# Hybrid encoder block on one core: down projection with tokens as rows, and projections of the merge in the wide form

## The chip, the cores and the metric

The kernel runs on one core of a Trainium2 chip. The metric is the device time of a run in microseconds. The engines are TensorE (PE, matmuls; PEld its weight loads), VectorE (DVE), ScalarE (ACT), GpSimd (POOL) and SyncE (SP), whose queue issues nearly all DMAs. Each works through its own list of instructions in order and waits on semaphores for the others.

## The reference

One layer over 256 tokens of width 2048, all in float32 (the weights and norms are drawn wider than here, which changes no shape):

```python
h = rms_norm(x, norm1_g)
proj = h @ w_in                      # u_a, v_a, feat_b, gate_a, gate_b
y_a = sgu_mixer(u_a, v_a, ...)       # spatial gating, width 1024
y_b = rwkv_mixer(feat_b, ...)        # two RWKV-7 scans, width 1024
merged = sigmoid(gate_a) * (y_a @ w_proj_a) + sigmoid(gate_b) * (y_b @ w_proj_b)
x = x + merged @ w_out
h2 = rms_norm(x, norm2_g)
gt = dwconv3_centred(h2 @ ffn_w_gate, ffn_conv_w, ffn_conv_b)
x = x + (silu(gt) * (h2 @ ffn_w_up)) @ ffn_w_down      # 5632 -> 2048
return rms_norm(x, norm_f_g)
```

## The kernel before

Activations lie feature by feature: a tile holds 128 features on the partitions and the 256 tokens as columns (P = 128, T = 256, KT = 16 tiles of the width 2048, FT = 44 of the width 5632, NP = 8 of the width 1024). Every large product is a *job* (`push`, L185): one tile of 128 output features, summed over nk tiles of input features. Its weights come in *chunks* of four 128x128 blocks, 256 KB each, which SP loads into a tile raw (`load_to`, L209).

To keep float32 precision with the faster fp32r matmul, each operand is the sum of a high and a low part. For the weights `split_to` (L216) makes them: ACT casts raw into hl[:, 0] (L223), DVE writes the rest into hl[:, 1] (L224). Activations are split in the same way when they are made (`split`, L172, and `split_scaled`, L176). `advance` (L228) takes one chunk at a time: it splits HL_AHEAD = 3 chunks ahead and issues the matmuls of the chunk, with the weights as the stationary and the activations as the moving operand. Low times low is left out. There are two forms:

- wide: high weights times high and low activations side by side (512 columns, L242), then low weights times high activations (256 columns, L246); two weight loads for 768 columns. The two halves of the result are added afterwards by `evac_sum` (L255: ACT copy L258, DVE add L259).
- narrow: three matmuls of 256 columns into one half (L244 to L246); three weight loads, nothing to add afterwards.

PE's work is thus one long row of jobs, and the rest of the kernel runs beside it in callbacks (`done`), called when a job's last matmul is issued. The stages, in order: projections of w_in with the RWKV and SGU work interleaved (wide; the gates' results, and branch A's times its gate, go to DRAM as spill); then the *merge*: the branch-B projection w_pb (16 jobs of 8 units, narrow, `done_b` L953) makes mg, the output projection w_out (16 jobs of 16 units, narrow, `done_o` L1007) adds x and makes h2 and the sum of squares for its norm; gate and up projections (88 wide jobs, `done_g`, `done_u`) make act; the *down* projection w_d (16 jobs of 44 units, the last one narrow, `done_d` L1053) adds into x2, which stays feature by feature. A unit is one 128x128 block with its two or three matmuls.

The final norm needs the sum of squares over all features, that is over partitions and tiles: `sumsq_rstd` (L980) adds squares tile by tile and sums over the partitions by a matmul with ones (L989, L990); then come, for each half of the tokens, the reciprocal root (`rsqrt`, L162) as a tile of 128x128, three multiplies (L1066) and three output DMAs (L1068).

From the merge on, raw has 8 buffers (RAW2) and is loaded 6 chunks ahead. The tile framework orders the instructions of each engine by its own estimates, so where a callback's work stands among the casts and subtracts of hl is not what the source alone shows.

## Time and profile before

| | us |
|---|---|
| median of 3 runs | 1582.59 (1581.76 to 1582.97) |
| profiled execution, its own time | 1567.25 |
| its span, first to last instruction | 1565.5 |
| PE busy in it | 1531.2 (98%) |
| DVE, ACT, POOL busy | 1222.2, 922.6, 37.9 |
| mean granted clock of TensorE | 0.996 |

The profile is one execution under the hardware profiler. Its spans on PE are pipelined: a matmul's duration overlaps the next one's, so a rate is read from the distance between starts. "Idle before" names what released an engine that had waited. The stages after the RWKV work lie, in us from the start of the span, at about 676 to 725 (branch B), 725 to 815 (output projection), 815 to 1304 (gate and up), 1304 to 1549 (down), and 1549 to the end (norm and output).

### The profile page before, as it was taken

Reading aid. Unit: us, or ns where it says so; the run is one execution under the profiler, and the core shown is the slowest. Engines: PE = TensorE matmul, PEld = TensorE weight load, DVE = VectorE, ACT = ScalarE, POOL = GpSimd, SP = SyncE. Lnnn points to the kernel's source line nnn. Section 1 sums busy time; section 2 is a strip of 40 time slices with the busy share of each in tenths; the row PEclk is TensorE's granted clock in tenths of the full one; section 3 lists DMA queues with packets and bytes.
Section 4 is the critical chain, followed back from the end, with each engine's and each line's share of the span. In section 5 each row is a group of like instructions: output and inputs, shape, how many; then the busy total and the mean of one; then the engine's idle time right before and its main releaser. Section 6 shows DMA issues by size and latency. Waiting matters only on the chain.

```text
span 1565.5 us, 35582 instructions
## 1 busy us (share of the span) xinstructions
PE 1531.2 (98%) x13420; PEld 1333.2 (85%) x13420; DVE 1222.2 (78%) x2500; ACT 922.6 (59%) x1920; POOL 37.9 (2%) x65
## 2 busy tenths in 40 slices
PE   6999999999999999999999999999999999999996
PEld 5888888888888878899998888888888888888885
DVE  8879998889898897687678777777787776555554
ACT  5667765665666655555556666666666665545452
POOL 2000000000000000000000000000000000000000
PEclk9999999999999999999999999999999999999998
DMA  6555553443443433597555555555555556666663
GB/s 230 195 181 177 166 160 126 132 144 120 135 140 116 139 100 124 161 316 240 187 182 188 194 190 189 189 192 190 190 189 189 190 191 191 189 191 190 190 190 100
DMA packets 151500, 273.72 MB, mean 175 GB/s; under 512 B 16928, under 2 KB 23200, under 8 KB 151328
## 3 DMA queue, kind: packets, MB, share of 16 engines
q1 hardware_dynamic: 148624, 263.91, 53.2%
q0 software_dynamic: 2560, 7.34, 1.4%
q8 instruction: 105, 1.72, 0.4%
q14 instruction: 67, 0.55, 0.1%
q10 hardware_dynamic: 144, 0.19, 0.0%
HBM read 265.09 MB, written 6.29 MB: 173 GB/s over the span
## 4 chain that ended last, share of the span: by engine, by line
PE 84%; issue 9%; DVE 4%; DMA 1%; ACT 1%; POOL 0%; SPq 0%; DVEq 0%; ACTq 0%; POOLq 0%
PE mm L242 45%; PE mm L246 26%; PE mm L244 3%; PE mm L245 3%; PE gp L669 1%; PE tp L717 1%; PE ms L541 1%; DVE hl L224 1%; DVE FQ L695 1%; PE tp L707 1%; PE cc L800 0%; DMA xt<-in_xT_dram 0%; PE tp L728 0%; DMA spill<-ev 0%; POOL spill L877 0%
## 5 line engine op out<-in xcount | busy, mean ns | idle before, releaser
L242 PE MATMUL mm<-h,hl 128*128 128x512 f32 x2624 | 935.7, 399 | 8.3 <-DVE h L178 7.6
L224 DVE TENSOR_TENSOR hl<-raw,hl 128x512 fp32r<-128x512 f32 x960 | 655.9, 689 | 231.0 <-ACT hl L223 227.3
L223 ACT CAST hl<-raw 128x512 fp32r<-128x512 f32 x960 | 594.7, 621 | 398.5 <-PE mm L246 284.9
L246 PE MATMUL mm<-h,hl 128*128 128x256 f32 x2624 | 733.3, 279 | 4.8 <-DVE hl L224 4.8
L242 PEld LDWEIGHTS mm<-h,hl 128*128 128x128 f32 x2624 | 493.2, 188 | 122.4 <-ACT hl L223 8.1
L246 PEld LDWEIGHTS mm<-h,hl 128*128 128x128 f32 x2624 | 495.0, 189 | 7.9 <-DVE hl L224 7.1
L242 PE MATMUL mm<-act,hl 128*128 128x512 f32 x660 | 228.8, 394 | 0.0
L246 PE MATMUL mm<-act,hl 128*128 128x256 f32 x704 | 195.3, 277 | 0.0
L242 PEld LDWEIGHTS mm<-act,hl 128*128 128x128 f32 x660 | 123.8, 188 | 28.7
L258 ACT COPY ev<-mm 128x256 f32<-128x256 f32 x180 | 67.1, 373 | 119.0 <-PE mm L246 118.7
L246 PEld LDWEIGHTS mm<-act,hl 128*128 128x128 f32 x704 | 132.4, 188 | 0.0
L259 DVE TENSOR_TENSOR ev<-mm,ev 128x256 f32<-128x256 f32 x180 | 75.9, 422 | 45.5 <-ACT ev L258 44.7
L246 PE MATMUL mm<-mg,hl 128*128 128x256 f32 x256 | 71.9, 281 | 0.0
L244 PE MATMUL mm<-mg,hl 128*128 128x256 f32 x256 | 71.7, 280 | 0.0
L245 PE MATMUL mm<-mg,hl 128*128 128x256 f32 x256 | 71.2, 278 | 0.0
L242 PE MATMUL mm<-ya,hl 128*128 128x512 f32 x128 | 48.2, 409 | 0.0
L244 PEld LDWEIGHTS mm<-mg,hl 128*128 128x128 f32 x256 | 48.1, 188 | 0.0
L245 PEld LDWEIGHTS mm<-mg,hl 128*128 128x128 f32 x256 | 48.1, 188 | 0.0
L246 PEld LDWEIGHTS mm<-mg,hl 128*128 128x128 f32 x256 | 48.1, 188 | 0.0
L1035 ACT ACTIVATE gt<-cp,colt 128x256 f32<-128x256 f32 x44 | 26.5, 603 | 19.1 <-DVE cp L1033 19.1
L246 PE MATMUL mm<-ybs,hl 128*128 128x256 f32 x128 | 36.2, 283 | 0.0
L245 PE MATMUL mm<-ybs,hl 128*128 128x256 f32 x128 | 36.2, 283 | 0.0
(285 smaller groups left out, 1523.6 us busy)
## 6 DMA issues: line engine op xcount, KB each, us to landing
raw<-in_w_in_dram SPq DMA_DIRECT2D x304, 256.0 KB, 3.0
raw<-in_w_g_dram SPq DMA_DIRECT2D x176, 256.0 KB, 3.1
raw<-in_w_u_dram SPq DMA_DIRECT2D x176, 256.0 KB, 2.9
raw<-in_w_d_dram SPq DMA_DIRECT2D x176, 256.0 KB, 2.9
raw<-in_w_out_dram SPq DMA_DIRECT2D x64, 256.0 KB, 3.0
raw<-in_w_pa_dram SPq DMA_DIRECT2D x32, 256.0 KB, 2.9
raw<-in_w_pb_dram SPq DMA_DIRECT2D x32, 256.0 KB, 4.7
spill<-ev POOLq DMA_DIRECT2D x32, 128.0 KB, 3.2
```

Source lines behind the costliest of these rows:

```text
L223: A.copy(hl[:, 0, :m], raw[:, s0:s0 + m])
L224: V.tensor_tensor(out=hl[:, 1, :m], in0=raw[:, s0:s0 + m], in1=hl[:, 0, :m].bitcast(F32), op=ALU.subtract)
L242: PE.matmul(ps[:, 0:512], hl[:, 0, j], a.rearrange("p a t -> p (a t)"), start=(k == 0), stop=False)
L244: PE.matmul(ps[:, 0:256], hl[:, 0, j], a[:, 0], start=(k == 0), stop=False)
L245: PE.matmul(ps[:, 0:256], hl[:, 0, j], a[:, 1], start=False, stop=False)
L246: PE.matmul(ps[:, 0:256], hl[:, 1, j], a[:, 0], start=False, stop=(k == job["nk"] - 1))
L258: A.copy(t, ps[:, 256:512])
L259: V.tensor_tensor(out=t, in0=ps[:, 0:256], in1=t, op=ALU.add)
L541: PE.matmul(ps[:, 0:T], bones, b[:, o], start=(o == 0), stop=(o == 1))
L669: PE.matmul(gps[hh][:, c * P:(c + 1) * P], BK[rows, d, c, hh:hh + 2, :].rearrange("p a b -> p (a b)"), AR[rows, d, c].rearrange("p a b -> ...
L695: V.copy_predicated(out=FQ2[qs, d, :, 1, :], mask=m2[qs, None, :].to_broadcast([32, NC, 32]), data=Gs[d][qs, q // 2, :, 0, b0:b0 + 32])
L1035: A.activation(gt, b[:, 1:T + 1], AF.Identity, scale=col("cw1", f), bias=col("cb", f))
```

## The change

The narrow form is given up in the merge: the jobs of w_pb and w_out are wide now, and `done_b` adds the halves with `evac_sum`.

The down projection turns its operands round. The activations act, a tile of 128 tokens at a time, become the stationary operand, and the split weights hl the moving one, 512 output features wide (WN): `push_tok` and `tok_mm`. A column group n of four takes 44 chunks, one per k; for each chunk there are three matmuls for token tile 0 and three for token tile 1, into two PSUM tiles pd0 and pd1. In the last group, token tile 1 runs up to LAG = 8 chunks behind token tile 0. The weights are laid out for this on the host, still 2 KB per partition and load.

The residual for the last addition must then have tokens as rows. x2 is no longer one tile for all features but six rotating ones, and `turn` transposes each of them on PE into x2t (two 128x128 transposes and one ACT copy per output job). `done_d` adds a result of 128x512 into x2t, squares it on ACT with a sum along the row, and lets GpSimd multiply by the norm's weights gf, which are loaded as one broadcast over the partitions. With the last group's result, the reciprocal root of a token tile is nine operations on one column (`rstd_of`); then ACT scales 768 columns and DVE 512 and 768, and two DMAs store the token tile.

RAW2 falls from 8 to 6, so 4 chunks are loaded ahead. The tiles h of the first projection are freed before the merge, and its small pools lie there. From the down projection on, hl has 4 + 9 buffers.

```diff
-RAW2 = 8
+RAW2 = 6
+
+WN = 512
+LAG = 8
+HL2 = 9
...
+    def push_tok(wd, nk, act, done, lag):
+
+
+        job = dict(wd=wd, nk=nk, act=act, done=done, ps=None, last=0, tok=True, lag=lag, at=0)
+        for k in range(nk):
+            raws.append([job, k, HK, None])
+            chunks.append([job, len(raws) - 1, 0, HK, None])
+        job["last"] = len(chunks)
+        jobs.append(job)
+        return job
+
+    def tok_mm(job, i):
+
+        if job["ps"] is None:
+            job["ps"] = [ps_d.tile([P, WN], F32, name=f"pd{t}", tag=f"pd{t}") for t in range(2)]
+        nk = job["nk"]
+        first = job["last"] - nk
+
+        def mm(t, k):
+            w = chunks[first + k][4].rearrange("p a b c -> p a (b c)")
+            a, ps, ts = job["act"](k), job["ps"][t], slice(t * P, t * P + P)
+            PE.matmul(ps, a[:, 0, ts], w[:, 0], start=(k == 0), stop=False)
+            PE.matmul(ps, a[:, 0, ts], w[:, 1], start=False, stop=False)
+            PE.matmul(ps, a[:, 1, ts], w[:, 0], start=False, stop=(k == nk - 1))
+            if k == nk - 1:
+                job["done"](t, ps)
+
+        k = i - first
+        mm(0, k)
+        upto = nk if k == nk - 1 else k + 1 - min(job["lag"], (k + 3) // 4)
+        while job["at"] < upto:
+            mm(1, job["at"])
+            job["at"] += 1
...
+            if r[0]["tok"]:
+                nc.sync.dma_start(r[3].rearrange("p a b -> p (a b)"), r[0]["wd"][:, r[1]])
+            else:
+                nc.sync.dma_start(r[3][:, :r[2]], r[0]["wd"][:, r[1]:r[1] + r[2]])
...
-            hl = hl_p.tile([P, 2, HK, P], F32R, name="hl", tag="hl")
+            hl = pools["hl"](ptr["hl"]).tile([P, 2, HK, P], F32R, name="hl", tag="hl")
...
+            if job["tok"]:
+                ptr["mm"] += 1
+                tok_mm(job, i)
+                continue
...
+    es_h.close()
...
-    x2 = xp_.tile([P, KT, T], F32, name="x2")
+
+    x2t = xp_.tile([P, 2, D], F32, name="x2t")
+    gf = xp_.tile([P, D], F32, name="gf")
+    ss = xp_.tile([P, 2, 8], F32, name="ss")
+    ps_d = ctx.enter_context(tc.tile_pool(name="ps_d", bufs=2, space=PSUM))
+    h2p = es_h2.enter_context(tc.tile_pool(name="h2p", bufs=1, reuse_waits="tile", side="right"))
+    h2 = [h2p.tile([P, 2, T], F32R, name=f"h2{m}") for m in range(KT)]
...
+            x2[m] = mgr.tile([P, T], F32, name="x2", tag="x2", bufs=X_AHEAD + 3)
+            nc.sync.dma_start(x2[m], xT[:, m])
...
-        V.scalar_tensor_tensor(out=sb, in0=sb, scalar=1.0, in1=ps, op0=ALU.add, op1=ALU.mult)
+        V.scalar_tensor_tensor(out=sb, in0=sb, scalar=1.0, in1=evac_sum(ev, ps), op0=ALU.add, op1=ALU.mult)
...
-        last_b = push(w_pb[m], NP, lambda k: ybs[k], lambda ps, m=m: done_b(m, ps), False)
+        last_b = push(w_pb[m], NP, lambda k: ybs[k], lambda ps, m=m: done_b(m, ps))
...
-        last_o = push(w_out[m], KT, lambda k: mg[k], lambda ps, m=m: lt["o"](m, ps), False)
+        last_o = push(w_out[m], KT, lambda k: mg[k], lambda ps, m=m: lt["o"](m, ps))
...
-    for m in range(KT):
-        last_d = push(w_d[m], FT, lambda k: lt["act"][k], lambda ps, m=m: lt["d"](m, ps), m < KT - 1)
+    ND = D // WN
+    for n in range(ND):
+        last_d = push_tok(w_d[n], FT, lambda k: lt["act"][k], lambda t, ps, n=n: lt["d"](n, t, ps),
+                          LAG if n == ND - 1 else 0)
...
+    def turn(m):
+
+        tp = ps_t2.tile([P, 512], F32, name="xt2", tag="xt2")
+        for t in range(2):
+            PE.transpose(tp[:, t * P:(t + 1) * P], x2[m][:, t * P:(t + 1) * P], ident)
+        A.copy(x2t[:, :, m * P:(m + 1) * P], tp[:, 0:T].rearrange("p (a b) -> p a b", a=2))
...
+        if m > 0:
+            turn(m - 1)
...
+    advance(2)
+    turn(KT - 1)
...
-        rf = actp.tile([P, T], F32, name="rf_")
-        add3, fin3 = sumsq_rstd(ev2, rf, NORM_EPS)
-
-        def done_d(m, ps):
-            for o in range(ps.shape[-1] // T):
-                V.tensor_tensor(out=x2[:, m], in0=ps[:, o * T:(o + 1) * T], in1=x2[:, m], op=ALU.add)
-            add3(m, x2[:, m])
-            if m > 0:
-                A.activation(x2[:, m - 1], x2[:, m - 1], AF.Copy, scale=col("norm_f_g", m - 1))
+        def rstd_of(t):
+
+            tot, s, y, u = (ss[:, t, 4 + i:5 + i] for i in range(4))
+            V.tensor_reduce(out=tot, in_=ss[:, t, 0:ND], axis=mybir.AxisListType.X, op=ALU.add)
+            V.tensor_scalar(out=s, in0=tot, scalar1=1.0 / D, scalar2=NORM_EPS, op0=ALU.mult, op1=ALU.add)
+            rsqrt(y, s, u)
+            return y
+
+        def done_d(n, t, ps):
+            xs, g = x2t[:, t, n * WN:(n + 1) * WN], gf[:, n * WN:(n + 1) * WN]
+            V.tensor_tensor(out=xs, in0=ps, in1=xs, op=ALU.add)
+            sq = ev2.tile([P, WN], F32, name="sqd", tag="sqd")
+            A.activation(sq, xs, AF.Square, accum_out=ss[:, t, n:n + 1])
+            if n < ND - 1:
+                G.tensor_tensor(out=xs, in0=xs, in1=g, op=ALU.mult)
+                return
+
+            r = rstd_of(t)
+            h = 3 * WN // 2
+            A.activation(x2t[:, t, 0:h], x2t[:, t, 0:h], AF.Copy, scale=r)
+            nc.sync.dma_start(out[t][:, 0:h], x2t[:, t, 0:h])
+            V.scalar_tensor_tensor(out=xs, in0=xs, scalar=r, in1=g, op0=ALU.mult, op1=ALU.mult)
+            V.tensor_scalar(out=x2t[:, t, h:2 * h], in0=x2t[:, t, h:2 * h], scalar1=r, scalar2=None, op0=ALU.mult)
+            nc.sync.dma_start(out[t][:, h:D], x2t[:, t, h:D])
...
+        nc.sync.dma_start(gf, norm_f.to_broadcast([P, D]))
+        finish(last_u)
+
+        es_h2.close()
+        hl2 = ctx.enter_context(tc.tile_pool(name="hl2", bufs=HL2, side="right"))
+        pools["hl"] = lambda i: hl_p if i % (4 + HL2) < 4 else hl2
...
-        A.activation(x2[:, KT - 1], x2[:, KT - 1], AF.Copy, scale=col("norm_f_g", KT - 1))
-        for ts in (slice(0, P), slice(P, T)):
-            fin3(ts)
-            m = 0
-            for n in (2, 6, 8):
-                V.tensor_tensor(out=x2[:, m:m + n, ts], in0=x2[:, m:m + n, ts],
-                                in1=rf[:, None, ts].to_broadcast([P, n, P]), op=ALU.mult)
-                nc.sync.dma_start(out[:, m:m + n, ts], x2[:, m:m + n, ts])
-                m += n
```

**How the order moves.** Three places. The first is ACT's list around the start of the merge (ybs are the split results of branch B, which its projection reads; hl<-raw is the cast of a chunk of weights). Before:

```order
L223 CAST hl<-raw 128x512
L882 ACTIVATE ev<-ev 128x256
L223 CAST hl<-raw 128x512
L173 CAST ybs_9926<-yb_116 128x256
...
L173 CAST ybs_9933<-yb_123 128x256
L258 COPY ev<-mm 128x256
L223 CAST hl<-raw 128x512 x4
```

Now:

```order
L264 CAST hl<-raw 128x512
L928 ACTIVATE ev<-ev 128x256
L264 CAST hl<-raw 128x512
L303 COPY ev<-mm 128x256
L264 CAST hl<-raw 128x512 x4
L177 CAST ybs_9952<-yb_116 128x256
...
L177 CAST ybs_9959<-yb_123 128x256
L303 COPY ev<-mm 128x256
```

The eight casts of ybs stood ahead of four casts of weights and now stand behind them.

The second is PE's list at the end of the second output job, now (mg are the merged activations, xt the transposes' PSUM tile, x the rotating x2):

```order
L287 MATMUL mm<-mg_9951,hl 128x512
L291 MATMUL mm<-mg_9951,hl 128x256
L1068 MATMUL xt_10815<-cst,x_10600 128x128 x2
L287 MATMUL mm<-mg_9936,hl 128x512
L291 MATMUL mm<-mg_9936,hl 128x256
```

Two transposes stand between two jobs, and a unit has two matmuls where it had three.

The third is the end of PE's list, now (pd_18757 is pd0 of the last column group, token tile 0; pd_18758 is pd1, token tile 1):

```order
L223 MATMUL pd_18757<-hl,act_11831 128x512
L224 MATMUL pd_18757<-hl,act_11831 128x512
L225 MATMUL pd_18757<-hl,act_11831 128x512
L223 MATMUL pd_18758<-hl,act_11823 128x512
L224 MATMUL pd_18758<-hl,act_11823 128x512
L225 MATMUL pd_18758<-hl,act_11823 128x512
...
L225 MATMUL pd_18758<-hl,act_11831 128x512
```

Token tile 0 takes the last k (act_11831), and token tile 1 follows with nine k from act_11823 on.

## Rows read from the trace of the kernel before

**Rows 1.** The page, part 1: busy us (share of the span) and instructions of each engine.

```profile
PE 1531.2 (98%) x13420; PEld 1333.2 (85%) x13420; DVE 1222.2 (78%) x2500; ACT 922.6 (59%) x1920; POOL 37.9 (2%) x65
```

**Rows 2.** Table by stretches: window, its length, PE, PEld, DVE, ACT, POOL, clock, DMA, GB/s.

```profile
671.00:725.00 54.00, 52.82 (x423) 51.56 (x422) 46.56 (x97) 32.07 (x65) 1.08 (x2) 1.00 0.91 304
725.00:815.00 90.00, 90.00 (x767) 90.00 (x766) 61.97 (x111) 50.96 (x95) 0.00 (x0) 1.00 0.57 188
...
1549.20:1565.50 16.30, 1.12 (x4) 0.32 (x3) 8.28 (x23) 0.92 (x2) 0.00 (x0) 0.61 0.48 129
```

**Rows 3.** Timeline of PE in the down stage: start us, duration us, instruction.

```profile
1449.66 0.39 PE L242 MATMUL mm<-act,hl 128*128 128x512 f32 x1
1449.89 0.27 PE L246 MATMUL mm<-act,hl 128*128 128x256 f32 x1
1450.01 0.40 PE L242 MATMUL mm<-act,hl 128*128 128x512 f32 x1
```

**Rows 4.** Instructions that read act: count, ns min/median/max, first and last start.

```profile
L242 PE MATMUL mm<-act,hl x660: 392/394/395, 1304.4 to 1532.9; 128*128 128x512 f32 x165
...
L244 PE MATMUL mm<-act,hl x44: 278/283/283, 1533.2 to 1548.7; 128*128 128x256 f32 x44
```

**Rows 5.** The same for line L244, in the two stages of the merge.

```profile
L244 PE MATMUL mm<-mg,hl x256: 280/280/284, 724.8 to 814.9; 128*128 128x256 f32 x128
...
L244 PE MATMUL mm<-ybs,hl x128: 279/283/283, 678.7 to 724.4; 128*128 128x256 f32 x128
```

**Rows 6.** Timeline of PE just ahead of the merge (last gate job).

```profile
675.45 0.28 PE L246 MATMUL mm<-h,hl 128*128 128x256 f32 x1
676.32 0.50 PE L242 MATMUL mm<-h,hl 128*128 128x512 f32 x1 [0.59 <-ACT hl L223]
677.41 0.38 PE L246 MATMUL mm<-h,hl 128*128 128x256 f32 x1 [0.59 <-DVE hl L224]
```

**Rows 7.** The end: timeline at the last matmul, and the output line L1068.

```profile
1548.92 0.28 PE L246 MATMUL mm<-act,hl 128*128 128x256 f32 x1
...
1549.23 0.42 DVE L1054 TENSOR_TENSOR x<-mm,x 128x256 f32<-128x256 f32 x1 [4.41 <-PE mm L246]
...
L1068 SPq DMA_DIRECT2D out_dram<-x x6: 372/502/1163, 1554.4 to 1558.9; - x6
...
DMA to landing us min/median/max: 1.9/3.6/4.7
```

**Rows 8.** Instructions on raw in the down stage (1304 to 1549).

```profile
L224 DVE TENSOR_TENSOR hl<-raw,hl x174: 679/692/694, 1303.9 to 1544.1; 128x512 fp32r<-128x512 f32 x174
L223 ACT CAST hl<-raw x173: 603/622/625, 1304.9 to 1543.5; 128x512 fp32r<-128x512 f32 x173
...
DMA to landing us min/median/max: 2.7/2.9/4.4
```

**Rows 9.** Timeline of DVE at the start of the merge: start, duration of the merged row.

```profile
673.66 2.76 DVE L174 TENSOR_TENSOR ybs<-yb,ybs 128x256 fp32r<-128x256 f32 x8
...
677.61 1.28 DVE L224 TENSOR_TENSOR hl<-raw,hl 128x512 fp32r<-128x512 f32 x2
```

**Rows 10.** Timeline of PE around a pair of transposes in the first stage.

```profile
86.30 0.28 PE L246 MATMUL mm<-h,hl 128*128 128x256 f32 x1
86.42 0.38 PE L440 MATMUL sgt<-cst,vu 128*128 128x128 f32 x2
...
86.87 0.28 PE L246 MATMUL mm<-h,hl 128*128 128x256 f32 x1
```

**Rows 11.** Timeline of DVE at the start of the kernel: its smallest operations.

```profile
6.49 0.17 DVE L145 TENSOR_SCALAR c<-c 128x28 f32<-128x28 f32 x1
6.57 0.16 DVE L152 TENSOR_SCALAR rkh<-colt 128x8 f32<-128x8 f32 x1
```

**Rows 12.** DMA queues from 1557.6 to 1559.6 us, while the output leaves.

```profile
DMA packets 1141, 0.57 MB, mean 285 GB/s; under 512 B 29, under 2 KB 1141, under 8 KB 1141
...
q1 hardware_dynamic: 1141, 0.57, 106.6%
```

More of the change, by code (lines that the diff above doesn't have):

```diff
@@ L117, in hybrid_kernel @@
 def hybrid_kernel(ctx: ExitStack, tc: tile.TileContext, xT, w_in, w_pa, w_pb, w_out, w_g, w_u, w_d,
-                  cols, consts, lora, sgu_wT, sgu_b, out):
+                  cols, consts, lora, sgu_wT, sgu_b, norm_f, out):
     nc = tc.nc
@@ L185, in push @@
     def push(wd, nk, act, done, wide=True):
-        job = dict(wd=wd, nk=nk, act=act, done=done, wide=wide, ps=None, last=0)
+        job = dict(wd=wd, nk=nk, act=act, done=done, wide=wide, ps=None, last=0, tok=False)
         for k0 in range(0, nk, RK):
@@ L263, in hybrid_kernel @@
     hl_p = ctx.enter_context(tc.tile_pool(name="hl", bufs=4))
+    pools["hl"] = lambda i: hl_p
     ev = ctx.enter_context(tc.tile_pool(name="ev", bufs=2))
     drp = ctx.enter_context(tc.tile_pool(name="drp", bufs=1, space=bass.MemoryType.DRAM))
-    es_mid, es_ya, es_f, es_mg = ExitStack(), ExitStack(), ExitStack(), ExitStack()
+    es_mid, es_h, es_ya, es_f, es_h2, es_mg = (ExitStack() for _ in range(6))
     mid = es_mid.enter_context(tc.tile_pool(name="mid", bufs=1))
-    hp = es_mid.enter_context(tc.tile_pool(name="hp", bufs=1))
+    hp = es_h.enter_context(tc.tile_pool(name="hp", bufs=1))
     fpool = es_f.enter_context(tc.tile_pool(name="fpool", bufs=1, side="right"))
@@ L939, in hybrid_kernel @@
     xp_ = ctx.enter_context(tc.tile_pool(name="x2p", bufs=1, reuse_waits="tile", side="right"))
-    x2 = xp_.tile([P, KT, T], F32, name="x2")
+    x2t = xp_.tile([P, 2, D], F32, name="x2t")
[4 more added lines that the diff above has]
+    h2 = [h2p.tile([P, 2, T], F32R, name=f"h2{m}") for m in range(KT)]
+    rstd2 = xp_.tile([P, T], F32, name="rstd2")
     mgr = es_mg.enter_context(tc.tile_pool(name="mgr", bufs=1, reuse_waits="tile", side="right"))
@@ L976, in hybrid_kernel @@
     es_mid.close()
-    h2p = ctx.enter_context(tc.tile_pool(name="h2p", bufs=1, reuse_waits="tile"))
-    h2 = [h2p.tile([P, 2, T], F32R, name=f"h2{m}") for m in range(KT)]
     def sumsq_rstd(pool, dst, n_eps):
@@ L1001, in sumsq_rstd @@
         return add, fin
-    rstd2 = h2p.tile([P, T], F32, name="rstd2")
+    es_t2 = ExitStack()
+    ps_t2 = es_t2.enter_context(tc.tile_pool(name="ps_t2", bufs=1, space=PSUM))
     add2, fin2 = sumsq_rstd(h2p, rstd2, NORM_EPS)
+    def turn(m):
[3 more added lines that the diff above has]
+        A.copy(x2t[:, :, m * P:(m + 1) * P], tp[:, 0:T].rearrange("p (a b) -> p a b", a=2))
     def done_o(m, ps):
@@ L1008, in done_o @@
         for o in range(ps.shape[-1] // T):
-            V.scalar_tensor_tensor(out=x2[:, m], in0=ps[:, o * T:(o + 1) * T], scalar=0.5, in1=x2[:, m],
+            V.scalar_tensor_tensor(out=x2[m], in0=ps[:, o * T:(o + 1) * T], scalar=0.5, in1=x2[m],
                                    op0=ALU.mult, op1=ALU.add)
-        split_scaled(h2[m], x2[:, m], col("norm2_g", m))
-        add2(m, x2[:, m])
+        split_scaled(h2[m], x2[m], col("norm2_g", m))
+        add2(m, x2[m])
+        if m > 0:
+            turn(m - 1)
     lt["o"] = done_o
@@ L1113, in _lay_out @@
         w_in=_block(w_in), w_pa=_block(l0("w_proj_a")), w_pb=_block(l0("w_proj_b")), w_out=_block(l0("w_out")),
-        w_g=_block(l0("ffn_w_gate")), w_u=_block(l0("ffn_w_up")), w_d=_block(l0("ffn_w_down")),
+        w_g=_block(l0("ffn_w_gate")), w_u=_block(l0("ffn_w_up")), w_d=np.ascontiguousarray(l0("ffn_w_down").reshape(FT, P, D // WN, WN).transpose(2, 1, 0, 3)),
         cols=cols, consts=build_constants(),
@@ L1131 @@
         args[name] = nc.dram_tensor(f"in_{name}_dram", a.shape, mybir.dt.from_np(a.dtype), kind="ExternalInput").ap()
-    args["out"] = nc.dram_tensor("out_0_dram", (P, KT, T), F32, kind="ExternalOutput").ap()
+    args["out"] = nc.dram_tensor("out_0_dram", (2, P, D), F32, kind="ExternalOutput").ap()
     with tile.TileContext(nc) as tc:
@@ L1136 @@
     o = r.results[0]["out_0_dram"]
-    return np.ascontiguousarray(o.transpose(1, 0, 2).reshape(D, T).T)[None]
+    return o.reshape(1, T, D)
```

9 lines of the change are left out of this document (5 added, 4 removed).

## The prediction

> **What bounds the kernel now.** I read the page first: TensorE (PE) is busy 98% of the span [rows 1]. Then the table by stretches [rows 2]: from the merge on PE is full in the stretches shown at a granted clock of 1.00 (the 2.4 GHz level), and the last 16.3 us hold almost no PE work. So up to the last matmul PE is the path, and behind it a tail counts in full. Three questions follow. What does PE pay per column in each form of matmul? What is missing before the merge? What does the tail consist of?
>
> *The wide form.* In the down stage a 512-column matmul is followed after 0.23 us, a 256-column one after 0.12 [rows 3]. 660 wide units begin between 1304.4 and 1532.9 [rows 4]: 228.5/659 = 346.7 ns for a unit of 768 columns, or 0.4514 ns per column (768 columns at 2.4 GHz would be 320 ns).
>
> *The narrow form.* Three matmuls of 256: 128 units of the branch-B projection take (724.4 - 678.7)/127 = 359.8 ns, 256 units of the output projection (814.9 - 724.8)/255 = 353.3, the 44 of the last down job (1548.7 - 1533.2)/43 = 360.5 [rows 4, 5].
>
> *The start of the merge.* PE starts two matmuls of the last gate job late: 0.87 us after a 256-column one and 1.09 us after a 512-column one instead of 0.12 and 0.23 [rows 6], 1.6 us lost, waiting for hl.
>
> *The tail.* From the start of the last down matmul at 1548.92 to the end at 1565.5: 16.6 us. It is the add, the sum over partitions, 14 small operations for two halves, six multiplies and six output DMAs, the last issued at 1558.9, landing 4.7 us later; some 1.9 us of closing follow [rows 7].
>
> **The change, part by part** (minus is faster; all against the span of 1565.5 and own time of 1567.25 of the one profiled execution; the runs' median, 1582.59, lies 15.3 above it, and I carry the difference over unchanged).
>
> 1. *Down stage on PE.* Before: 704 units, from 1304.4 [rows 4] to the last start at 1548.9 [rows 7], 244.5 us. After: 4 column groups x 44 k x 2 token tiles x 3 = 1056 matmuls of 512 columns; the columns, 540,672, are the same. The trace has no run of 512-column matmuls one after the other. By the rate per column one costs 512 x 0.4514 = 231.1 ns, and it is also what passes between a 512-column matmul and the next one now (0.23). 1055 x 0.2311 = 243.8: **-0.7**. Bounds: if the 26.7 ns over 320 are a fixed sum per matmul, 13.3 each, one costs 226.7 and the stage 239.2, -5.3. If moving data that ACT and DVE have just written costs the slowest rate per column in these rows, 120 per 256, it is 240 ns and 253.2 us, +8.7. I take the rate per column, because the two spacings now stand as 2 to 1.
>    Its cover: per chunk ACT and DVE still do one cast (622 ns) and one subtract (692) against 6 x 0.231 = 1.39 us of PE, as today; a raw load lands in 2.9 us [rows 8], and the ring of 6 with 4 ahead is 5.5 us of PE. The six GpSimd multiplies lie a column group (61 us) ahead of whoever reads them. I cost these at nothing; with the ring too short PE would wait for raw chunk by chunk.
>
> 2. *Wide form in the merge.* 128 x (359.8 - 346.7) = **-1.7**; 256 x (353.3 - 346.7) = **-1.7**. Each of the 32 jobs gains an ACT copy and a DVE add. In the branch-B jobs (8 units, 2.77 us) DVE then does two subtracts and four operations of 256 columns. By durations that is 2 x 0.69 + 4 x 0.42 = 3.06, over 2.77; but operations overlap: eight take 2.76 us (0.345 each), two subtracts 1.28 [rows 9], so 1.28 + 4 x 0.345 = 2.66. DVE just fits; I take the full gain, and the bound is the sum by durations, 16 x 3.06 = 49.0 against 46.1 today, +2.9 in place of -1.7.
>
> 3. *Transposes to token rows.* Two per output job, 32 in all. The existing pair of this shape (sgt) stretches a wide unit from 0.35 us to 0.57 (86.30 to 86.87) [rows 10]: 16 x 0.22 = **+3.5**. Their ACT copy (some 0.4) is covered: ACT works 51 of 90 us there [rows 2]. The DMAs of x now wait for a transpose, some five jobs ahead of their use; the raw loads queued behind on SP have the ring.
>
> 4. *Start of the merge.* The order shows ACT doing the four casts of hl ahead of the eight of ybs instead of behind. ybs then begins when the third of the last gate job's four chunks is done, 1.39 us ahead of the first use; the first one needs a last cast of hl (0.65), its own (0.35), and a subtract behind the subtract of hl (0.69 + 0.42), 1.8 us with waits. So 0.4 us of stall in place of 1.6: **-1.2**. Bounds -1.6 and +2: the 1 MB broadcast of the norm weights moves ahead of raw loads on SP's queue (3.4 us at the 304 GB/s of this stretch [rows 2]); ten loads of x, 1.3 MB, leave the stretch. What is behind it needs its data eight chunks later.
>
> 5. *Tail.* After the last 512-column matmul starts: 0.43 to the add (0.31 today, plus 0.12 for the longer matmul); add of 512 columns 0.69, square 0.62; nine operations on 128x1 at 0.16 (rows of 8 and 28 columns [rows 11]) 1.44; multiply of 512 and of 768 columns, 0.70 + 0.95 less overlap, 1.6 (ACT's 768 beside it, shorter); five handovers 0.25; the DMA of 640 KB behind 384 KB, 4.5 (512 KB take 4.7 when queued [rows 7]); closing 1.9. Sum 11.4 against 16.6: **-5.2**. Token tile 0 goes out earlier: behind its last matmul PE has nine lagged steps of three, 27 x 0.231 = 6.2 us. Bounds: landing 2.9 to 6 us, small operations 0.08 (their spacing) to 0.17: -3.6 to -7.5.
>
> Sum: -0.7 - 3.4 + 3.5 - 1.2 - 5.2 = -7.0, or **1582.6 - 7.0 = 1575.6**.
>
> **Rivals.**
> A. *A fixed cost per matmul, not per column.* 1056 matmuls replace 1452. For: narrow units, three matmuls on the same columns, cost more (353 to 360). Against: 0.23 and 0.12 is the columns' ratio. It gives the down stage -5.3, the sum -11.6: 1571.0.
>    The Trainium skill's "TensorE: Matmul & The Clock Gate", section "Back-to-back issue gap", has a rule of this kind: columns over 2.4 plus 2.5 ns, so 215.8 for 512. By that rule the new down stage would be an estimated 227.7 us, and the sum -23.1. The trace does not agree for the wide unit: the rule gives 325, rows 3 and 4 show 346.7.
> B. *The streamed operand is slower.* The down stage's moving data now come from hl, which ACT and DVE write until shortly before; today they are tiles written long ago. Each ns per matmul costs 1.06 us, so the gain is gone from 237.7 ns and the kernel slower by over 0.2% from 240.8. At 240: -7.0 + 9.4 = +2.4, 1585.0. For: no row shows such a read. Against: weight loads read hl now without a visible wait.
> C. *DVE bounds the branch-B jobs*, and the wide form gains nothing there: +2.9 in place of -1.7, 1580.2. For: 46.6 of 54 us busy [rows 2]. Against: the overlap [rows 9].
> D. *The tail doesn't get shorter than its output.* 2 MB leave at 285 GB/s at the end today, the queue 106.6% busy [rows 12]. If token tile 0 isn't out by the end of PE, all of it follows: half the gain of 5.2 goes, 1578.2.
>
> **How the numbers follow.** Forecast 0.50, A 0.17, B 0.11, C 0.14, D 0.08. A measurement here tells about 0.2% (3.2 us) from no change, so faster means under 1579.4 and slower over 1585.8. Forecast, A and D are nearly all faster (0.69 of 0.75), C to a quarter: 0.72. Slower is B's upper half with C and a short raw ring: 0.08. The rest, 0.20, is no change. The range leaves out the lower part of A and the upper part of B: 1568.5 to 1584.5.
>
> **What would show it.** After: no wait of PE over 0.5 us around the start of the merge; 346.7 ns per unit in both merge stages, with 0.22 more per pair of transposes; starts of the down matmuls 0.231 apart and the stage 244 us; 11 to 12 us from the last matmul's start to the end. A down stage at 239 or below is A, one over 250 B, waits of PE for hl in the branch-B jobs C. I am wrong if PE waits for raw loads in the down stage or the last DMA lands more than 6 us after its issue.

## The result, and the profile after

The changed kernel takes 1562.86 us (median of 4 runs, 1562.55 to 1566.96), the kernel before beside it 1582.78 (4 runs, 1581.76 to 1584.15). The ratio is 0.9879, 95% interval [0.9865, 0.9893]: 20 us faster. The forecast was 1575.6 with a range of 1568.5 to 1584.5; the time lies below it. The profiled execution of the changed kernel took 1562.55 and spans 1560.4 us, so it belongs to the timed runs. That of the kernel before (1567.25, span 1565.5) did not belong to its own: it was 15.3 us shorter than the median, and this turned out to be the point.

The page of the changed kernel, part 1, and its table by stretches (columns as in [rows 2]):

```profile
PE 1530.1 (98%) x12668; PEld 1304.7 (84%) x12668; DVE 1220.1 (78%) x2495; ACT 922.5 (59%) x1938; POOL 48.5 (3%) x71
```

```profile
671.00:725.00 54.00, 52.17 (x300) 45.13 (x299) 49.93 (x112) 35.55 (x81) 1.08 (x2) 1.00 0.86 292
725.00:815.00 90.00, 90.00 (x531) 80.03 (x530) 67.81 (x126) 54.05 (x109) 0.32 (x1) 1.00 0.60 200
1550.30:1560.40 10.10, 0.15 (x1) 0.00 (x0) 3.39 (x12) 1.66 (x3) 0.00 (x0) 0.63 0.42 167
```

PE has 752 instructions fewer, and 1.1 us less busy time than [rows 1]. The stretch behind the last product is 10.1 us long instead of 16.3. PE's instructions by tile in the changed kernel (count, ns min/median/max, first and last start), which answer to [rows 4, 5]; line 287 is the 512-column product of a wide unit, line 223 the first of the three products of a row of weights in the down stage:

```profile
L287 PE MATMUL mm<-mg,hl x256: 390/390/480, 724.0 to 815.6; 128*128 128x512 f32 x128
...
L287 PE MATMUL mm<-ybs,hl x128: 392/395/466, 677.9 to 723.7; 128*128 128x512 f32 x128
...
L287 PE MATMUL mm<-h,hl x1408: 389/390/481, 816.5 to 1305.2; 128*128 128x512 f32 x176
...
L223 PE MATMUL pd<-hl,act x352: 389/394/402, 1305.6 to 1549.6; 128*128 128x512 f32 x176
```

In the end the chain of the second token tile stands alone (timeline, as [rows 7]):

```profile
1550.06 0.39 PE L225 MATMUL pd<-hl,act 128*128 128x512 f32 x1
1550.49 0.69 DVE L1129 TENSOR_TENSOR x2t<-pd,x2t 128x512 f32<-128x512 f32 x1 [1.78 <-PE pd L225]
1551.21 0.63 ACT L1131 ACTIVATE sqd<-x2t 128x512 f32<-128x512 f32 x1 [2.79 <-DVE x2t L1129]
...
1553.70 0.75 DVE L1140 SCALAR_TENSOR_TENSOR x2t<-x2t,ss,gf 128x512 f32<-128x512 f32 x1
...
1555.15 0.38 SPq L1142 DMA_DIRECT2D out_dram<-x2t  x1
```

### The profile page after: what moved, and what is told of

Read it like the earlier page. It is cut to its first block, busy times and chain, and to the rows that moved or that the text cites. A ratio compares the mean times of both kernels' runs of the same rounds, so it can differ in the third digit from the quotient of the medians.

```text
span 1560.4 us, 34079 instructions
## 1 busy us (share of the span) xinstructions
PE 1530.1 (98%) x12668; PEld 1304.7 (84%) x12668; DVE 1220.1 (78%) x2495; ACT 922.5 (59%) x1938; POOL 48.5 (3%) x71
## 4 chain that ended last, share of the span: by engine, by line
PE 90%; DVE 5%; ACT 2%; issue 1%; DMA 1%; DVEq 0%; ACTq 0%; SPq 0%
PE mm L287 43%; PE mm L291 22%; PE pd L223 5%; PE pd L225 5%; PE pd L224 5%; PE gp L715 1%; PE tp L763 1%; PE ms L587 1%; DVE hl L265 1%; PE tp L753 1%; DVE FQ L741 1%; PE cc L846 1%; DMA sab<-spill 0%; PE tp L774 0%; ACT hl L264 0%
## 5 line engine op out<-in xcount | busy, mean ns | idle before, releaser
L303 ACT COPY ev<-mm 128x256 f32<-128x256 f32 x196 | 73.2, 374 | 124.3 <-PE mm L291 122.5
L223 PE MATMUL pd<-hl,act 128*128 128x512 f32 x352 | 138.8, 394 | 0.0
L225 PE MATMUL pd<-hl,act 128*128 128x512 f32 x352 | 138.5, 393 | 0.0
L224 PE MATMUL pd<-hl,act 128*128 128x512 f32 x352 | 138.4, 393 | 0.0
L304 DVE TENSOR_TENSOR ev<-mm,ev 128x256 f32<-128x256 f32 x196 | 82.7, 422 | 46.1 <-ACT ev L303 44.9
L287 PE MATMUL mm<-mg,hl 128*128 128x512 f32 x256 | 90.7, 395 | 0.0
L225 PEld LDWEIGHTS pd<-hl,act 128*128 128x128 f32 x352 | 66.0, 188 | 15.7
L223 PEld LDWEIGHTS pd<-hl,act 128*128 128x128 f32 x352 | 66.0, 188 | 15.4
L224 PEld LDWEIGHTS pd<-hl,act 128*128 128x128 f32 x352 | 66.0, 188 | 15.4
L291 PE MATMUL mm<-mg,hl 128*128 128x256 f32 x256 | 72.1, 282 | 0.0
L287 PEld LDWEIGHTS mm<-mg,hl 128*128 128x128 f32 x256 | 48.1, 188 | 9.7
L291 PEld LDWEIGHTS mm<-mg,hl 128*128 128x128 f32 x256 | 48.4, 189 | 0.0
L287 PE MATMUL mm<-ybs,hl 128*128 128x512 f32 x128 | 44.8, 396 | 1.8 <-ACT ev L303 1.4
L291 PE MATMUL mm<-ya,hl 128*128 128x256 f32 x128 | 36.0, 281 | 0.0
```

Source lines behind the costliest of these rows:

```text
L223: PE.matmul(ps, a[:, 0, ts], w[:, 0], start=(k == 0), stop=False)
L224: PE.matmul(ps, a[:, 0, ts], w[:, 1], start=False, stop=False)
L225: PE.matmul(ps, a[:, 1, ts], w[:, 0], start=False, stop=(k == nk - 1))
L287: PE.matmul(ps[:, 0:512], hl[:, 0, j], a.rearrange("p a t -> p (a t)"), start=(k == 0), stop=False)
L291: PE.matmul(ps[:, 0:256], hl[:, 1, j], a[:, 0], start=False, stop=(k == job["nk"] - 1))
L303: A.copy(t, ps[:, 256:512])
```

## The experiments

The first question was where 20 us come from when a sum against the profiled execution gave 7. "Quick" and "slow" below are the two values that one kernel shows from execution to execution.

### The kernel before, profiled again

> The kernel before, unchanged. The profiled execution of before took 1567.25 us, its timed runs 1582.6; the changed kernel's profiled and timed runs agree (1562.55 and 1562.86). Theory 1 (the 15 us lie in the executions of before: it has a slower course that its one profiled execution missed): this run's executions spread over 1567 and 1582, and the trace of one near 1582 shows where the 15 us lie. Theory 2 (the profiled execution was on a faster chip or day): all executions here lie within 3 us of one another, at one level. Theory 3 (the profiler itself takes 15 us off this kernel): profiled 1567, timed 1582 again.

1582.48 (11 runs, 1581.16 to 1583.44), ratio 0.9998 [0.9989, 1.0007]; this time the profiled execution took 1582.96 and spans 1581.1. Its products by tile: line 242 has the 512-column ones of the wide units, line 244 a product of each narrow unit in the merge, line 246 the last one of every unit:

```profile
L242 PE MATMUL mm<-h,hl x1408: 391/398/586, 817.4 to 1315.3; 128*128 128x512 f32 x176
...
L242 PE MATMUL mm<-act,hl x660: 395/398/403, 1315.7 to 1548.5; 128*128 128x512 f32 x165
...
L244 PE MATMUL mm<-mg,hl x256: 280/280/284, 726.7 to 816.8; 128*128 128x256 f32 x128
...
L244 PE MATMUL mm<-ybs,hl x128: 283/283/283, 680.6 to 726.3; 128*128 128x256 f32 x128
...
L246 PE MATMUL mm<-act,hl x704: 277/281/284, 1315.9 to 1564.6; 128*128 128x256 f32 x176
```

In the down stage a unit of 768 columns takes (1548.5 - 1315.7)/659 = 353.3 ns, where the quick execution had 346.7 [rows 4]; in the gate and up stage the same. PE waits for nothing in either, and the granted clock of both stages is 1.00 in both executions. 1408 + 660 units of 6.67 ns are 13.8 us. The narrow units of the output projection take 353.3 in both executions [rows 5]. The two profiled executions lie 15.7 us apart: 13.8 are a slower pace of PE's stream of products from 817 us up to the last down job, and 1.9 are a later start of branch B (680.6 instead of 678.7). So the 15.3 us are not a constant beside the kernel. The later start is not tied to the pace: over the traces of this study branch B starts between 677.8 and 681.9 us, in quick and in slow executions alike. By stages, with the changed kernel (us, between first starts; the tail from the last start of the down stage):

| | before, quick [rows] | before, slow | changed |
|---|---|---|---|
| up to branch B | 678.7 | 680.6 | 677.9 |
| branch B | 46.1 | 46.1 | 46.1 |
| output projection, to the first gate product | 90.7 | 90.7 | 92.5 |
| gate and up | 488.9 | 498.3 | 489.1 |
| down | 244.5 | 248.9 | 244.5 |
| tail | 16.6 | 16.5 | 10.3 |
| span | 1565.5 | 1581.1 | 1560.4 |

Against a quick execution the change brings 5.1 us, against a slow one 20.7. What remains is why the changed kernel was quick in every run.

### Each half of the change alone

In the kernel before, both merge projections wide (`False` removed from the two `push` calls, `evac_sum(ev, ps)` in done_b):

> The kernel before with one part of the change: the branch-B and output projections in the wide form, everything else as before. By the traces of before and after (branch B 360 ns per unit in both, output projection 353 to 345.5) the path shortens by 2 us: 1580.6 if before is at 1582.6. Theory 1a (what makes before slow in some executions lies in the narrow matmuls of the merge): 1565 to 1568. Theory 1b (it lies in the down stage or the end): 1580 to 1583.

1565.37 (4 runs, 1564.85 to 1566.36), ratio 0.9891 [0.9876, 0.9906]. The changed kernel with the merge narrow again (both `push` calls with `False`):

> The changed kernel with the merge's two projections in the narrow form again; token rows in the down projection, the transposes, the new end, the shorter raw ring stay. By the traces: the output projection costs 2 us more than in the changed kernel: 1565. Theory 1a (narrow matmuls of the merge make the slow executions): 1575 to 1583. Theory 1b (the old down stage or end makes them): 1563 to 1567.

1569.15 (4 runs, 1568.91 to 1569.50), ratio 0.9915 [0.9901, 0.9929]. Both theories missed here: the narrow merge did not bring the slow value (1a), and the time lies above 1b's 1563 to 1567, since branch B takes 51.2 us in this trace (678.9 to 730.1) with a stop of PE of 2.9 us in it; of such stops more below. Either half alone takes some 13 to 17 us off, and the two together 20: both bring the quick pace, and it counts once. The wide merge alone shows it, and shows branch B at the full gain that I had forecast:

```profile
L242 PE MATMUL mm<-act,hl x660: 391/391/391, 1303.2 to 1531.7; 128*128 128x512 f32 x165
...
L242 PE MATMUL mm<-ybs,hl x128: 391/391/391, 681.1 to 725.1; 128*128 128x512 f32 x128
```

(725.1 - 681.1)/127 = 346.5 ns, and 346.7 in the down stage.

### Is the pace kept, and what changes it

```
 (the kernel before, in done_u)
             split(act[f], u)
+            if f == 10:
+                tp = ps_ms.tile([P, 512], F32, name="ms", tag="ms")
+                for t in range(2):
+                    PE.transpose(tp[:, t*P:(t+1)*P], x2[:, 0, t*P:(t+1)*P], ident)
```

> The kernel before, with one pair of unread PE transposes of x2[0] put behind up projection 10 (a quarter into the gate and up stage); nothing else. Theory P (the pace of the wide units is fixed by how PE comes into the stage, and holds until PE's stream is broken): units of 353.3 ns up to the break as in the repeated run of before, and another pace behind it; if that is 346.7 ns, the 34 features left and the down projection (1088 + 660 units) take 6.7 ns less each, 11.7 us, and the time is about 1571. Rival Q (the slow pace belongs to what the narrow merge leaves behind, or to the run, and not to PE's stream): 353.3 on both sides and 1582.7.

1582.05 (10 runs, 1571.77 to 1584.62), ratio 0.9992 [0.9966, 1.0017]; the kernel before beside it 1568.62 to 1583.71, 2 of its 24 runs quick. The profiled execution (span 1579.6) came into the stage quick. Line 242 before and behind the pair of transposes, which starts at 940.76 between two units:

```profile
L242 PE MATMUL mm<-h,hl x318: 391/394/396, 829.8 to 939.7; 128*128 128x512 f32 x159
```

```profile
940.76 0.38 PE L1051 MATMUL ms<-cst,x 128*128 128x128 f32 x2
```

```profile
L242 PE MATMUL mm<-h,hl x1006: 394/398/404, 944.9 to 1300.0; 128*128 128x512 f32 x168
```

109.9/317 = 346.7 ns ahead of it, 355.1/1005 = 353.3 behind it, and so to the end. That is the opposite direction of what I wrote, but it is the mechanism: in this execution one short interruption of a wide stream moved PE to another pace, which it then kept through 1700 units. Rival Q would have one pace throughout and is out. Two of the ten runs, 1571.77 and 1572.46, lie near the 1571 that I expected for a step the other way; no trace shows what they did.

### Which seam

```
 (e4)  w_out: push(..., lt["o"](m, ps), False)  ->  push(..., lt["o"](m, ps))
 (e5)  w_pb:  push(..., done_b(m, ps), False)   ->  push(..., done_b(m, ps)), evac_sum in done_b
 (e6)  both wide, and w_out with  m < KT - 1  as its last argument
```

> The kernel before with the output projection alone in the wide form; branch B stays narrow. Theory P: PE enters the gate and up stage from a wide stream as in the run with both wide, so units of 346.7 ns there: 1582.5 - 13.8 - 1.7 = 1567. Rival Q' (the branch B stage decides, since it comes first): 353.3 stays, only the merge's own 1.7 us are won: 1580.8.

1567.08 (4 runs, 1566.98 to 1567.77), ratio 0.9901 [0.9886, 0.9916].

> The kernel before with branch B alone in the wide form; the output projection stays narrow. Theory P: the seam ahead of the gate and up stage is as before, narrow, so 353.3 ns stays there: 1582.5 - 1.7 = 1580.8. Rival Q' (branch B decides): 346.7 from there on, about 1567.

1580.58 (10 runs, 1568.24 to 1582.68; two quick), ratio 0.9973 [0.9951, 0.9994].

> Both merge projections wide as in the run with both, but the last of the 16 output projections narrow again. Theory P: PE comes into the gate and up stage through a narrow stream as before, and its units take 353.3 ns: 1565.4 + 13.8 = 1579. If the entry needs more of the narrow form than its last 48 matmuls, or if the form ahead is not what decides: 1565.5.

1567.22 (8 runs: six of 1564.38 to 1567.71, two of 1579.28 and 1580.02), ratio 0.992 [0.9892, 0.9949]. So it is the seam from the output projection into the gate stage: branch B alone leaves the kernel with both values, the output projection alone settles it, and a single narrow job ahead of the seam brings the slow value back in two of eight (by their times; the traced execution was quick). That last result is not what theory P said (slow in all): with narrow products ahead of this seam the slow pace is possible, not certain.

### The kernel before with the changed kernel's transposes at the seam

```
     fin2()
+    advance(2)
+    tp = ps_ms.tile([P, 512], F32, name="ms", tag="ms")
+    for t in range(2):
+        PE.transpose(tp[:, t*P:(t+1)*P], x2[:, KT-1, t*P:(t+1)*P], ident)
```

> The kernel before (both merge projections narrow) with two products of gate job 0 brought ahead of a pair of unread transposes, at the place and in the manner in which the changed kernel turns its last x2 tile. Theory P, in the form the last four runs leave it (the pace of 346.7 or 353.3 ns per wide unit is settled by the first few products of the stage and then kept): the run with the merge narrow and this break in it had 346.7 in all four executions, so this one has it too: 1582.5 - 13.8 = 1568.7 in all or nearly all. Rival R (wide products or the other things of the changed kernel are needed, the break alone is not): most executions at 1582.7 as before.

1582.83 (10 runs, 1582.26 to 1584.10), while 23 of the 31 runs of the kernel before beside it, on that chip, were quick (median 1569.26). My expectation fell, and so did R as I had worded it: the transposes as such don't bring the quick pace, here they went with the slow one in all ten. In the traced execution the units were slow from 819.12 us on, ahead of the transposes at 820.54; why none of the ten was quick is open. The share of quick executions of the kernel before differs from chip to chip: none in 26 on one, 2 of 24, 23 of 31, 2 of 13 and 3 of 20 on the four others of the experiments.

What the kernels that were quick in every run had in common up to here was found in the seam itself. There PE does two pairs of products for the sum of squares, ms<-tot and ms<-sqn (one product for each half of the tokens). In the kernel before, and in each variant that had shown the slow value, ms<-sqn stands between two wide units, behind the 256-column product; in the changed kernel and the others that were always quick it stands inside a unit, behind the 512-column one. In the execution of 1582.96 us of the kernel before and in the changed kernel (timelines of PE):

```profile
818.50 0.28 PE L246 MATMUL mm<-h,hl 128*128 128x256 f32 x1
818.73 0.70 PE L990 MATMUL ms<-sqn,cst 128*128 128x256 f32 x2
819.08 0.58 PE L242 MATMUL mm<-h,hl 128*128 128x512 f32 x1
```

```profile
817.67 0.39 PE L287 MATMUL mm<-h,hl 128*128 128x512 f32 x1
817.96 0.70 PE L1047 MATMUL ms<-sqn,cst 128*128 128x256 f32 x2
818.31 0.47 PE L291 MATMUL mm<-h,hl 128*128 128x256 f32 x1
```

### One instruction of ACT in two

```
 (the kernel before, in sumsq_rstd)
-            A.activation(sq, src, AF.Square)
+            for cs in ((slice(0, P), slice(P, T)) if m == KT - 1 else (slice(0, T),)):
+                A.activation(sq[:, cs], src[:, cs], AF.Square)
```

> The kernel before with one ACT instruction in two: the squares of the last x2 tile go in two halves of 128 tokens. This moves the second product of the sum of squares (ms<-sqn) on PE by one place: from between two units of gate job 0 (behind the 256-column product) to inside one (behind the 512-column product). Theory P2 (that place settles the pace of what follows: inside a unit it is 346.7 ns, always; between two units it falls to 346.7 or 353.3 by a few ns): 1568.5 in every execution, also where the kernel before gives 1582.6 beside it. Rival R2 (it takes the wide form in the output projection, as all kernels had that were quick in every execution but one): as the kernel before on the same chip, 1582.6 in most or 1568.5 in most, with both values among its runs.

1568.74 (7 runs, 1568.14 to 1570.06), the kernel before beside it 1582.77 (2 of 13 quick): ratio 0.9922 [0.9900, 0.9944]. The seam and the stages of this kernel:

```profile
817.95 0.39 PE L242 MATMUL mm<-h,hl 128*128 128x512 f32 x1
818.18 0.68 PE L991 MATMUL ms<-sqn,cst 128*128 128x256 f32 x2
818.51 0.47 PE L246 MATMUL mm<-h,hl 128*128 128x256 f32 x1
```

```profile
L242 PE MATMUL mm<-act,hl x660: 391/391/391, 1305.5 to 1534.0; 128*128 128x512 f32 x165
```

346.7 ns per unit. Nothing of the change is in this kernel, and 14 of the 20 us are. Three runs ask whether it is the place or something else in the edit. In the first, the same squares go in four pieces (`cuts = (0, 64, 128, 192, 256)`), which moves ms<-sqn on to the next boundary:

> The kernel before with the squares of the last x2 tile in four ACT instructions. Beside the run with two halves this moves ms<-sqn one place further on PE, from inside unit 4 of gate job 0 to between units 4 and 5. Theory P2 (the place settles it): the slow pace is back in some or most executions, 1582.6, as in the kernel before on the same chip. Rival R3 (what made the run with halves quick is the finer ACT work, or the later moment, and not the place on PE): 1568.5 in all executions.

1582.52 (10 runs, 1569.26 to 1583.62; two quick), ratio 0.9991 [0.9963, 1.0020]. Its profiled execution:

```profile
819.06 0.28 PE L246 MATMUL mm<-h,hl 128*128 128x256 f32 x1
819.22 0.70 PE L992 MATMUL ms<-sqn,cst 128*128 128x256 f32 x2
819.57 0.58 PE L242 MATMUL mm<-h,hl 128*128 128x512 f32 x1
```

```profile
L242 PE MATMUL mm<-act,hl x660: 394/398/404, 1315.8 to 1548.7; 128*128 128x512 f32 x165
```

Finer work on ACT, and the slow pace is back; R3 is out. In the second, halves in the kernel with branch B wide, two of whose ten executions had been quick:

> The kernel before with branch B wide and the output projection narrow, which ran at 1568.3 in two of ten executions and at about 1581 in eight, now with the squares in two halves, so that ms<-sqn lies inside unit 4. Theory P2: 1568 or a little less in all executions. Rival R3 or chance: both values again.

1567.20 (9 runs, 1566.59 to 1568.73), ratio 0.9920 [0.9890, 0.9949]. The third is the kernel with the output projection wide, with three pieces (`cuts = (0, 64, 128, 256)`):

> The kernel before with the output projection wide (1567.1 in all four executions), and the squares of the last x2 tile in three pieces, which moves ms<-sqn from inside a unit of gate job 0 to between two. Theory P2: both values among its runs, 1567 and 1581, in a share that depends on the chip. Rival R2 (the wide form makes it quick): 1567.3 in all.

1566.06 (5 runs, 1565.57 to 1567.41), ratio 0.9920 [0.9877, 0.9962]: quick in all, so theory P2 was wrong in its second half: the place alone does not make the slow pace. R2 is what came, but the run is not a clean test of the form. Behind narrow products PE stood for a moment ahead of ms<-sqn wherever that pair lies between units (it starts 0.16 to 0.23 us behind the 256-column product, as above). Here it starts after the usual 0.12:

```profile
817.57 0.28 PE L246 MATMUL mm<-h,hl 128*128 128x256 f32 x1
817.69 0.70 PE L992 MATMUL ms<-sqn,cst 128*128 128x256 f32 x2
```

The same in the changed kernel, with halves:

> The changed kernel with the squares in two halves, which moves ms<-sqn from inside unit 4 to between units 4 and 5, one pair of transposes still behind it. If the place alone settles the pace: some executions 9.4 us longer, from the gate and up stage (1408 units of 6.7 ns), at 1572 to 1576. If the slow pace needs a narrow stream ahead of the place as well, as the run of the wide output projection with three pieces suggests (1566.1 in all five): as the changed kernel, 1562.5 to 1567.

1564.96 (6 runs, 1562.81 to 1566.56), ratio 0.9910 [0.9872, 0.9947]. In this run PE did stand for a moment ahead of ms<-sqn (it starts 0.16 us behind the 256-column product), but pairs of transposes stand on both sides of it. So at this seam only kernels with both showed the slow pace, narrow products ahead of it and ms<-sqn between units behind it. For a narrow stream the runs with halves and quarters show that moving ms<-sqn settles it (whether by the place as such or by that short stop they do not tell apart). That narrow products are needed as well is not shown, and in general they are not: the break above brought the slow pace into a wide stream, and whole wide stages of branch B ran at it with no narrow job anywhere ahead. In the traces of (e6), and of the run with the spill tiles in gf's buffer that closes the part on branch B below:

```profile
L242 PE MATMUL mm<-ybs,hl x128: 395/398/403, 681.9 to 726.7; 128*128 128x512 f32 x128
```

```profile
L287 PE MATMUL mm<-ybs,hl x128: 395/398/468, 678.7 to 723.7; 128*128 128x512 f32 x128
```

That is (726.7 - 681.9)/127 = 353 ns in the first and 354 in the second, where the kernel with both projections wide, the same as (e6) up to the last output job, had 346.5. At this seam the change takes both conditions away: its output projection is wide, and in its order on PE, with the projections wide or narrow, ms<-sqn lies inside a unit.

### The smaller terms

*Branch B.* The changed kernel's gain there was missing. Timeline of PE and of DVE at the one gap:

```profile
686.28 0.28 PE L291 MATMUL mm<-ybs,hl 128*128 128x256 f32 x1
687.91 0.47 PE L287 MATMUL mm<-ybs,hl 128*128 128x512 f32 x1 [1.35 <-ACT ev L303]
```

```profile
685.61 0.42 DVE L1016 SCALAR_TENSOR_TENSOR sab<-sab,ev 128x256 f32<-128x256 f32 x1 [1.86 <-DMA sab<-spill]
```

DVE stands 1.86 us at the first spill tile, with the subtracts of hl queued behind it, and PE then loses 1.5 us. Two edits:

```
 (e7)   gf = actp.tile(...) behind the merge, in place of xp_.tile(...) ahead of it
 (e10)  sab = gf[:, m % 4 * 2*T : (m % 4 + 1) * 2*T].rearrange("p (a t) -> p a t", a=2)
```

> The changed kernel with the row of the final norm's gains (gf, 1 MB into the chip) placed in a buffer that comes free only behind the merge, so that its load can't go ahead of the spill loads of branch B. In the changed kernel's trace PE stands still once for 1.3 us in branch B (the 512-column product of 686.28), which goes back over ACT's copy and DVE to a spill tile that landed 7.7 us after its issue. Theory S1 (gf's load holds up that spill load): it lands in about 5 us, the stall goes, and the time is 1562.8 - 1.3 = 1561.5. Rival S2 (the spill loads are late because their buffers lie where PE's last reads of h were): 1562.8, the stall stays.

1562.31 (10 runs, 1560.88 to 1563.86). The gap is gone from the trace, as S1 said and S2 did not: the spill tiles land in at most 6.3 us instead of 7.7, though the first is issued later, at 679.1 instead of 677.9. But S1's 1561.5 was not reached. Branch B starts at 679.0 instead of 677.9, and its units take (724.0 - 679.0)/127 = 354.3 ns on average, the slow pace, 0.9 us over 128 units. That the time is close to the 1562.86 of the changed kernel says little by itself, since that kernel itself differs by 3.7 us between two chips (below).

> The changed kernel with the spill tiles of branch B in gf's buffer, which is free from the start of the merge, so that the first four spill loads don't wait for PE's last reads of h; gf itself is loaded behind branch B. S1 and S2 both say that the stall of 1.3 us goes: 1561.5. If it stays, the wait is in the two buffers for ACT's copies of the upper half (ev), and the time is 1562.8.

1561.19 (10 runs, 1560.29 to 1561.73). The gap is gone here too. The changed kernel did not run on that chip, so both went to one:

> The changed kernel unchanged, to stand beside the next one on the same chip, and beside the kernel before where that may run at either pace: 1562.8 in all executions by theory P2, since its ms<-sqn lies inside a unit.

> The changed kernel with the spill tiles of branch B in gf's buffer once more, now beside the changed kernel on the same chip. S2: 1561.2, which is 1.5 below the changed kernel; if the gain was the chip's, no difference.

The changed kernel 1566.56 (6 runs, 1564.47 to 1567.11), with the spill tiles in gf's buffer 1562.72 (4 runs, 1562.20 to 1563.49): 3.8 us less, and the two sets don't overlap. My 1562.8 for the changed kernel was missed, because on this chip the wait was longer:

```profile
689.04 0.42 DVE L1016 SCALAR_TENSOR_TENSOR sab<-sab,ev 128x256 f32<-128x256 f32 x1 [3.39 <-DMA sab<-spill]
```

PE then stood for 2.96 us, and behind that the granted clock is 0.61 from 690 to 694 us: four units take 0.64 us each or more, at the 1.2 GHz level, before the clock is back at 1.00. That adds some 1.4 us to the stop (an estimate from these spacings):

```profile
691.34 0.76 PE L287 MATMUL mm<-ybs,hl 128*128 128x512 f32 x1 [2.96 <-DVE ev L304]
...
692.12 0.63 PE L287 MATMUL mm<-ybs,hl 128*128 128x512 f32 x1
```

The version with the spill tiles in gf's buffer is the fastest of the study, ahead of both kernels. Of the two causes, gf's load ahead on SP's queue is enough: with it gone the gap went, with the spill tiles where they had been in the program. What the buffer that PE's last reads of h hold costs by itself is not shown, since the second edit puts gf's load behind branch B as well.

*The tail.* The changed kernel with `0` in place of `LAG if n == ND - 1 else 0`:

> The changed kernel without the stagger at its end: the second token tile of the last 512 features follows the first at every row of weights, so the two tiles end 0.7 us apart instead of 5.5 or more. My step on the tail (the first tile's norm and output lie beside PE's last products): they now go with the second tile's; DVE alone has 4 us of them, and 1 MB more leaves after the last product at about 400 GB/s, 2.6 us. Time 1562.8 + 3 = 1565.8 (1564 to 1568). Rival: what the end waits for is the chain of the second tile alone, and the first hides beside it: 1563.

1566.39 (10 runs, 1563.99 to 1568.88). From the last product's start (1552.83) to the end (1565.1) it is 12.3 us in place of 10.3, so the stagger is worth 2.0, and not the 3 that I gave it. That the time still met my forecast is luck: the rest of the difference is not the tail, since in this trace PE waits 2.4 us in branch B and runs some units at the lower clock behind that.

## Why the prediction was wrong

The step that failed is the sentence ahead of the list: "the runs' median, 1582.59, lies 15.3 above it, and I carry the difference over unchanged". It treated as a constant what was a pace of PE, 353.3 ns against 346.7 per wide unit, 13.8 us in all, and a later merge (1.9). In all runs of the changed kernel the slow pace of these stages is gone, so the 13.8 us went with it. The terms themselves stand against a quick execution, where they gave -7.0 and the traces -5.1:

1. *Down stage on PE*: right. (1549.6 - 1305.6)/1053 = 231.7 ns per product of 512 columns; forecast 231.1, A's bound 226.7, B's 240. Both rivals are out. By the rule of the Trainium skill ("TensorE: Matmul & The Clock Gate", section "Back-to-back issue gap") it would be 215.8; the trace does not agree, and the measurement stands. The stage is 244.5 us in both kernels, so -0.7 became 0. The cover held: the products start at an even spacing to the end.
2. *Wide form in the merge*: right in the output projection, where with the transposes of term 3 the forecast was -1.7 + 3.5 = +1.8 and the traces show 92.5 against 90.7. Wrong in branch B: 0 in place of -1.7. Not by rival C, since the wide merge alone ran these jobs at 346.5 ns with the same work on DVE, but by one stop of 1.5 us at a spill tile. I had looked at the loads of raw and x moving in SP's queue, not at the spill loads that were moved behind them.
3. *Transposes*: right, as above.
4. *Start of the merge*: 677.9 against 678.7, -0.8 for -1.2. The mechanism held (PE stands 0.47 us there, forecast 0.4), but the start differs by more than this between executions.
5. *Tail*: mis-sized, 10.3 for 11.4, against 16.6 before: -6.3 for -5.2. I took 4.5 us for the last DMA; those of the two token tiles landed in these times (by line: KB each, median us from issue to landing):

```profile
out_dram<-x2t SPq DMA_DIRECT2D x2, 640.0 KB, 3.5
out_dram<-x2t SPq DMA_DIRECT2D x2, 384.0 KB, 2.4
```

D is out: the last output of token tile 0 was issued at 1548.85, ahead of PE's end, and without the stagger the tail is 2.0 longer.

The trace that I had could have warned: the same narrow unit took 359.8 ns in one stage and 353.3 in the next [rows 5], so the spacing of products was not a property of the product alone; and one profiled execution 1% under runs that agree to 0.1% was a difference to be explained, or at least a rival with a chance of its own. With "the change makes the slow pace go" among the cases the range would have reached to 1562.

Open are why a short interruption can lead into the slow pace, why at this seam it does so only between units and behind narrow products, what set the slow pace in branch B, and why chips differ in how often. The changed kernel with a narrow merge and ms<-sqn between units, where both conditions would come together again, was not tried.

## What to carry to other kernels

When a profiled execution and the timed runs of one kernel differ by more than the runs among themselves, don't carry the difference as a constant: compare the spacing of one repeated unit stage by stage in both, and give the case that the change touches it a chance. In a stream that PE never leaves, the place of a single small product at a seam can be worth more than a restructured stage: here a split of one ACT instruction gave 14 us and the rest of a large change 5. An edit that moves loads in a queue is costed for each load that it passes, above all for the one at which the engine stands that feeds PE.

## What had not been expected of the hardware

At a granted clock of 1.00 the same pair of products (512 and 256 columns) runs at 346.7 or at 353.3 ns, a third value of 359.8 to 360.5 showing for narrow units [rows 4, 5], and PE can keep a value for hundreds of microseconds. In the traces it changed at an interruption (the break in the gate and up stage; the stop in branch B of the changed kernel, whose 24 units ahead of it took 353 ns and those behind it 347), but also without one, where in (e6) the 353 ns of branch B gave way to 346.7 in the output projection. It shows in the spacing alone: in the quick executions the products follow each other after 0.23 and 0.12 us throughout, in the slow one in wider ones that differ from unit to unit. Timeline of PE in the kernel before, execution of 1582.96 us, in the gate and up stage:

```profile
1039.73 0.40 PE L242 MATMUL mm<-h,hl 128*128 128x512 f32 x1
1039.97 0.28 PE L246 MATMUL mm<-h,hl 128*128 128x256 f32 x1
1040.09 0.40 PE L242 MATMUL mm<-h,hl 128*128 128x512 f32 x1
1040.33 0.28 PE L246 MATMUL mm<-h,hl 128*128 128x256 f32 x1
1040.44 0.40 PE L242 MATMUL mm<-h,hl 128*128 128x512 f32 x1
1040.67 0.28 PE L246 MATMUL mm<-h,hl 128*128 128x256 f32 x1
1040.79 0.40 PE L242 MATMUL mm<-h,hl 128*128 128x512 f32 x1
```

From one 512-column product to the next it is 0.36, 0.35 and 0.35 us here, with 0.24, 0.24 and 0.23 behind the 512-column product.
